# A new opening for an encoder step: the first weight block in half-size pieces scaled on ScalarE, the gain vectors on ScalarE's queue, and the remaining loads ordered behind the query weights

## The chip, the cores and the metric

The kernel runs on one core of one Trainium2 chip. The metric is the device time of one execution in microseconds (us); lower is better. Engine names are those of the profile: PE is TensorE, PEld its weight loads, DVE is VectorE, ACT is ScalarE, POOL is GpSimd, SP is SyncE, which issues most DMAs.

## The reference, cut to what matters

One step of a two-layer streaming encoder over 1024 prompt tokens and 8 x 16 sample tokens, width 1024, all in float32. The opening of a layer is a norm, a projection, and a norm of each head:

```python
def rmsnorm(x, g):
    y = xf * lax.rsqrt(jnp.mean(xf * xf, axis=-1, keepdims=True) + EPS)
    return (y * g.astype(jnp.float32)).astype(x.dtype)

def project_a(x, g_norm, w_qkv, g_q, g_k):
    qkv = rmsnorm(x, g_norm) @ w_qkv
    q, k, v = jnp.split(qkv, [N_HEADS * HEAD_DIM, (N_HEADS + N_KV_HEADS) * HEAD_DIM], axis=-1)
    q = rmsnorm(q.reshape(b, t, N_HEADS, HEAD_DIM), g_q)
    k = rmsnorm(k.reshape(b, t, N_KV_HEADS, HEAD_DIM), g_k)
```

Layer A then does a sliding-window attention with learned sinks, an output projection and a squared-ReLU MLP; layer B does the same with a shared K/V projection (`w_kv`, norm gain `g_kv`), a query projection (`w_q_b`) and an attention over more tokens.

## The kernel before, in words

The tokens lie in nine tiles of 128: tiles 0 to 7 are the prompt and tile ST (number 8) is the sample. A float32 product is made of three float32r matmuls: each operand is split into a high part (a rounded copy) and a low part (the rest), and high x high, high x low and low x high are added in PSUM (lines 182 to 184, three matmuls for each of eight 128-row blocks of the contraction, called k0 to k7 here).

The norm is folded in. Its gain is multiplied into the weights: `load_block` loads a 1024 x 512 weight block in four raw tiles of 512 KB, each with two of the eight k, and `split_g` makes of each k the high part, scaled by the gain column `gcol` (POOL, line 152, since `"g"` is in the layer's `eng` string), and the low part (DVE, line 155). The token's own scale is applied after the product. `prep_gains` loads five gain vectors as rows, transposes them on PE (line 1139) and copies them to `gcol` (DVE, line 1140). It has a PSUM pool of its own and runs ahead of everything else.

The names of the steps of a layer's attention (`attention`): `X(t)` loads tile t (line 1313). `N(t)` transposes it on PE (eight 128 x 128 transposes, line 175), splits the result into `hh` and `hl` (ACT line 109, DVE line 115) and makes the statistics (ACT line 166, DVE lines 167 and 1144, POOL line 1148). `K1(t)` is the key and value projection with the first weight block, `wkv`; its end (`kv_stage1`, lines 233 to 262) empties the PSUM tile with ACT (lines 241, 248, 249) and DVE (line 242). `K2(t)` transposes the keys (`ps_q<-ks`) and splits them into `KT`, of which two DMAs (lines 278, 279) make a swapped copy. `Q1(t, nb)` is the query projection with the second weight block (`wq[0]`); its end (`q_stage1`) makes `qn` and `qr` on ACT (lines 191, 192), and a power on POOL and a product on DVE (lines 203, 204) finish `qr`. In layer A there is one buffer of `qr`, in layer B two. `Q2(t, nb)` transposes `qr` into `qT`. `spill(t)` stores `hh` and `hl` to DRAM as `hTd` (line 1343), and `R(t)` reads them back much later. `sinks` loads the constant table `cst` and the sinks and makes five small DVE tiles of them (lines 1238 to 1256). `unit` works on the sample's caches (`kc`, `vc`). Layer A starts with tiles 0, 1 and ST, whose `K1` are woven k by k into three PSUM tiles; that of tile 0 is the only buffer of its kind ("m") and is used again by `Q1(0)`.

Nothing of the order is fixed by hand here: the tile framework's scheduler lists the instructions of each engine by a simulated timeline, starting from the order and the priorities in which they are written, so a change of the written order moves instructions elsewhere too. Each engine then runs its list strictly in order. DMAs of SP and of ACT share eight completion counters in turn; in the built program a DMA waits, on the engine that issues it, until the DMA that had the same counter before has landed, so about eight are in flight. `behind(a, b)` tells the scheduler to list b behind a; it adds no wait on the chip.

Of the kernel before, what the change touches and what calls it, by code (L numbers as in the profile page):

```python
# [75 lines left out]
class Build:  # L76
# [70 lines left out]
    def split_g(self, hi, lo, raw, g, k0):  # L147
        nc = self.nc
        for k in range(raw.shape[1]):
            s = self.gcol[:, g * KC + k0 + k : g * KC + k0 + k + 1]  # L150
            if "g" in self.engs:
                nc.gpsimd.tensor_scalar(hi[:, k], raw[:, k], s, 1.0, ALU.mult, ALU.mult)
# [2 lines left out]
            nc.vector.scalar_tensor_tensor(  # L155
                lo[:, k], raw[:, k], s, hi[:, k].bitcast(F32), ALU.mult, ALU.subtract
            )
# [20 lines left out]
    def proj(self, ps, ah, al, w, ks=range(KC)):  # L178
        nc = self.nc
        for k in ks:  # L180
            a, b = ah[k // 4][:, k % 4, :], al[k // 4][:, k % 4, :]
            nc.tensor.matmul(ps, a, w[:, 0, k, :], start=(k == 0), stop=False)  # L182
            nc.tensor.matmul(ps, a, w[:, 1, k, :], start=False, stop=False)  # L183
            nc.tensor.matmul(ps, b, w[:, 0, k, :], start=False, stop=(k == KC - 1))  # L184
# [943 lines left out]
    def prep_gains(self):  # L1128
        nc, I = self.nc, self.ins
        with ExitStack() as st:  # L1130
            self.psum_pools(st, "pg", dict(m=(1, 1)), dict(m="m"))
            tmp = self.pool(st, "tmpg")
            g = tmp.tile([5 * KC, P], F32, tag="g", name="g")
            for i, v in enumerate(
                (I["g_attn"][0], I["g_attn"][1], I["g_mlp"][0], I["g_mlp"][1], I["g_kv"])
            ):
                nc.sync.dma_start(g[i * KC : (i + 1) * KC, :], v.rearrange("(k p) -> k p", p=P))
            ps = self.psum("m", [P, 5 * KC], "ps_g")
            nc.tensor.transpose(ps, g, self.ident[0 : 5 * KC, 0 : 5 * KC])
            nc.vector.tensor_copy(self.gcol, ps)  # L1140
# [94 lines left out]
    def sinks(self, ring):  # L1235
        nc, I = self.nc, self.ins
        self.cst = ring.tile([P, C_W], F32, tag="cst", name="cst")
        nc.sync.dma_start(self.cst, I["consts"])
# [7 lines left out]
        for i in range(G):  # L1246
            nc.sync.dma_start(
                self.ssink[i * 32 : i * 32 + 32, :],
                sk[i : i + 13 : 4].partition_broadcast(32),
            )  # L1250
# [5 lines left out]
        nc.vector.tensor_tensor(self.susink, self.ssink, rsl, ALU.mult)  # L1256

    def attention(self, layer):
# [17 lines left out]
        with ExitStack() as st:  # L1276
# [27 lines left out]
            def X(t):  # L1304
                if A:
# [7 lines left out]
                nc.sync.dma_start(xr[t], x_src(t))  # L1313
# [475 lines left out]
```

## Time and profile before

| | |
|---|---|
| runs, median of 3 | 2394.24 us (2392.23 to 2396.98) |
| the profiled execution, its own time | 2396.21 us |
| its span in the trace, mean granted clock | 2394.4 us, 0.993 |
| busy shares | PE 97%, PEld 81%, DVE 68%, ACT 51%, POOL 23% |
| DMA | 385.88 MB, mean 161 GB/s |

The span runs from the first to the last instruction in the trace. PE is busy nearly all the time, so the places that matter are those in which PE waits or runs at a reduced clock. In a row of the timeline stand the start, the duration, the engine, the line, the operation with its output and inputs, the count of instructions merged, and in brackets the idle time just before with what ended it.

### The profile page before, as it was taken

Reading aid. Unit: us, or ns where it says so; the run is one execution under the profiler, and the core shown is the slowest. Engines: PE = TensorE matmul, PEld = TensorE weight load, DVE = VectorE, ACT = ScalarE, POOL = GpSimd, SP = SyncE. Lnnn points to the kernel's source line nnn. Section 1 sums busy time; section 2 is a strip of 40 time slices with the busy share of each in tenths; the row PEclk is TensorE's granted clock in tenths of the full one; section 3 lists DMA queues with packets and bytes.
Section 4 is the critical chain, followed back from the end, with each engine's and each line's share of the span. In section 5 each row is a group of like instructions: output and inputs, shape, how many; then the busy total and the mean of one; then the engine's idle time right before and its main releaser. Section 6 shows DMA issues by size and latency. Waiting matters only on the chain.

```text
span 2394.4 us, 33443 instructions
## 1 busy us (share of the span) xinstructions
PE 2315.4 (97%) x11621; PEld 1932.2 (81%) x11621; DVE 1629.9 (68%) x3002; ACT 1212.0 (51%) x2415; POOL 542.5 (23%) x836
## 2 busy tenths in 40 slices
PE   7999999899999999999999999998999999999999
PEld 6777877788888878888777788876888888888887
DVE  6787786755655767776577876877655555777674
ACT  3776675555555432332277666665555555323321
POOL 4343332312212100000243444444111211000000
PEclk9998999999999999999999999999999999999999
DMA  7345545344433874342754655555433445734332
GB/s 253 119 132 166 171 155 193 103 150 157 145 129 141 324 245 141 112 141 100 246 155 114 197 163 169 166 167 171 141 133 137 154 141 202 275 138 158 114 115 115
DMA packets 218393, 385.88 MB, mean 161 GB/s; under 512 B 50344, under 2 KB 125040, under 8 KB 211056
## 3 DMA queue, kind: packets, MB, share of 16 engines
q1 hardware_dynamic: 195152, 307.18, 39.0%
q0 software_dynamic: 21776, 71.84, 7.8%
q10 hardware_dynamic: 1296, 4.72, 0.5%
q8 instruction: 92, 1.51, 0.3%
q14 instruction: 77, 0.63, 0.1%
HBM read 246.47 MB, written 136.14 MB: 160 GB/s over the span
## 4 chain that ended last, share of the span: by engine, by line
PE 81%; DVE 7%; DMA 6%; ACT 3%; issue 2%; POOL 1%; SPq 0%; POOLq 0%; ACTq 0%; DVEq 0%
PE ps_x L711 9%; PE ps_x L713 9%; PE ps_x L712 9%; PE ps_y L713 7%; PE ps_y L712 7%; PE ps_y L711 7%; PE ps_mm L182 3%; PE ps_mm L184 3%; PE ps_mm L183 3%; PE ps_tr L289 2%; PE ps_mm L143 2%; PE ps_mm L145 2%; PE ps_mm L144 2%; PE ps_s L713 1%; PE ps_s L712 1%
## 5 line engine op out<-in xcount | busy, mean ns | idle before, releaser
L109 ACT CAST w<-r 128x2048 fp32r<-128x2048 f32 x56 | 107.1, 1913 | 321.6 <-PE ps_y L713 210.6
L711 PE MATMUL ps_x<-w,s 128*128 128x512 f32 x512 | 199.5, 390 | 4.3 <-DVE x L1017 2.2
L713 PE MATMUL ps_x<-w,s 128*128 128x512 f32 x512 | 199.4, 389 | 0.0
L712 PE MATMUL ps_x<-w,s 128*128 128x512 f32 x512 | 199.2, 389 | 0.0
L182 PE MATMUL ps_mm<-w,hh 128*128 128x512 f32 x432 | 174.2, 405 | 9.7 <-DMA hh<-hTd 3.3
L184 PE MATMUL ps_mm<-w,hl 128*128 128x512 f32 x432 | 174.1, 404 | 1.7 <-DMA hl<-hTd 1.6
L183 PE MATMUL ps_mm<-w,hh 128*128 128x512 f32 x432 | 172.5, 400 | 1.6 <-DVE w L155 1.6
L109 ACT CAST s<-s 128x2048 fp32r<-128x2048 f32 x56 | 107.2, 1914 | 121.3 <-DMA s<-hd 112.2
L115 DVE TENSOR_TENSOR w<-r,w 128x2048 fp32r<-128x2048 f32 x56 | 128.2, 2289 | 51.0 <-ACT w L109 51.0
L711 PE MATMUL ps_x<-sx,w 128*128 128x512 f32 (+1 forms) x408 | 157.9, 387 | 3.8 <-ACT hc L830 2.9
L1017 DVE TENSOR_TENSOR x<-ps_y,x 128x512 f32<-128x512 f32 x136 | 92.3, 687 | 99.8 <-PE ps_y L713 99.8
L713 PE MATMUL ps_x<-sx,w 128*128 128x512 f32 (+1 forms) x408 | 154.1, 378 | 0.0
L712 PE MATMUL ps_x<-sx,w 128*128 128x512 f32 (+1 forms) x408 | 154.1, 378 | 0.0
L109 ACT CAST w<-ru 128x512 fp32r<-128x512 f32 (+1 forms) x160 | 110.0, 708 | 85.4 <-PE ps_y L712 32.0
L713 PE MATMUL ps_y<-w,s 128*128 128x512 f32 x384 | 149.5, 389 | 0.0
L711 PE MATMUL ps_y<-w,s 128*128 128x512 f32 x384 | 149.4, 389 | 0.0
L712 PE MATMUL ps_y<-w,s 128*128 128x512 f32 x384 | 149.4, 389 | 0.0
L115 DVE TENSOR_TENSOR s<-s 128x2048 fp32r<-128x2048 f32 x56 | 128.0, 2286 | 30.4 <-ACT s L109 30.3
L115 DVE TENSOR_TENSOR ptl<-ps_tr,pth 128x512 fp32r<-128x512 f32 x180 | 122.6, 685 | 24.2 <-ACT pth L109 18.6
L115 DVE TENSOR_TENSOR w<-ru,w 128x512 fp32r<-128x512 f32 (+1 forms) x160 | 126.4, 792 | 11.2 <-ACT w L109 11.2
L115 DVE TENSOR_TENSOR wq<-ru,wq 128x1024 fp32r<-128x1024 f32 x32 | 39.7, 1240 | 132.2 <-ACT wq L109 132.2
L109 ACT CAST pth<-ps_tr 128x512 fp32r<-128x512 f32 x180 | 104.8, 595 | 45.6 <-PE ps_tr L289 33.2
(279 smaller groups left out, 6570.6 us busy)
## 6 DMA issues: line engine op xcount, KB each, us to landing
s<-hd SPq DMA_DIRECT2D x56, 1024.0 KB, 4.7
ru<-in_w_up SPq DMA_DIRECT2D x64, 512.0 KB, 3.8
r<-in_w_down SPq DMA_DIRECT2D x32, 1024.0 KB, 5.8
hd<-hc POOLq DMA_DIRECT2D x128, 256.0 KB, 2.7
hd<-hs POOLq DMA_DIRECT2D x96, 256.0 KB, 2.5
x<-xd SPq DMA_DIRECT2D x41, 512.0 KB, 4.5
o<-oTd SPq DMA_DIRECT2D x52, 256.0 KB, 3.9
hTd<-hh SPq DMA_DIRECT2D x36, 256.0 KB, 3.9
```

The source lines that it names most:

```text
L109: a = nc.scalar.copy(hi, src)
L115: return a, e.tensor_tensor(lo, src, hi.bitcast(F32), ALU.subtract)
L143: nc.tensor.matmul(ps, oh[:, k, :], w[:, 0, k, nn], start=(k == 0), stop=False)
L144: nc.tensor.matmul(ps, oh[:, k, :], w[:, 1, k, nn], start=False, stop=False)
L145: nc.tensor.matmul(ps, ol[:, k, :], w[:, 0, k, nn], start=False, stop=(k == 3))
L182: nc.tensor.matmul(ps, a, w[:, 0, k, :], start=(k == 0), stop=False)
L183: nc.tensor.matmul(ps, a, w[:, 1, k, :], start=False, stop=False)
L184: nc.tensor.matmul(ps, b, w[:, 0, k, :], start=False, stop=(k == KC - 1))
L711: a = mm(ps, ah, bh, start=first, stop=False, skip_group_check=True)
L712: mm(ps, ah, bl, start=False, stop=False, skip_group_check=True)
L713: return a, mm(ps, al, bh, start=False, stop=last, skip_group_check=True)
L1017: tt(xs[t][:, N[n]], ps, xs[t][:, N[n]], ALU.add)
```

## The change

In words:

- `prep_gains` is split up. `load_gains` issues three DMAs (two gain matrices at once, and `g_kv`) on ACT's queue; `turn_gains`, the transpose and the copy to `gcol`, is written behind `N(0)`.
- In layer A's first weight block each raw tile is loaded by two DMAs of 256 KB, one for each k, and its high part is made on ACT (`first=True`) and no longer on POOL.
- `X(0)` and `N(0)` are written ahead of the first weight load. The raw tile of ST's tokens lies in another pool (`qT`).
- `self.gate` names the last weight load (later the loads of tiles 2 and 3). The spills of tiles 0, 1 and ST, the loads of `cst`, the sinks, `kc`, `vc` and `gb` are listed behind it. `sinks` is written behind the `K1` steps, and its DVE operations are listed behind the last matmul of `proj`.
- `Q2(0, 0)` is written ahead of `K2(1)`, and in layer A `X(2)` and `X(3)` ahead of `spill(0)`. The move of `Q2(0, 0)`, and the gate on spills, caches and `gb`, hold for layer B as well.

```diff
-    def load_block(self, dst, w, n0, g, ks=range(0, KC, 2)):
+    def load_block(self, dst, w, n0, g, ks=range(0, KC, 2), first=False):
...
-            nc.sync.dma_start(raw, wr[:, k0 : k0 + 2, n0 : n0 + 512])
-            self.split_g(dst[:, 0, k0 : k0 + 2, :], dst[:, 1, k0 : k0 + 2, :], raw, g, k0)
+            step = 1 if first else 2
+            for k in range(0, 2, step):
+                self.gate = nc.sync.dma_start(
+                    raw[:, k : k + step], wr[:, k0 + k : k0 + k + step, n0 : n0 + 512]
+                )
+            self.split_g(dst[:, 0, k0 : k0 + 2, :], dst[:, 1, k0 : k0 + 2, :], raw, g, k0, first)
...
-            if "g" in self.engs:
+            if "g" in self.engs and not first:
                 nc.gpsimd.tensor_scalar(hi[:, k], raw[:, k], s, 1.0, ALU.mult, ALU.mult)
             else:
                 nc.scalar.activation(hi[:, k], raw[:, k], AF.Copy, scale=s)
...
-            nc.tensor.matmul(ps, b, w[:, 0, k, :], start=False, stop=(k == KC - 1))
+            self.lp = nc.tensor.matmul(ps, b, w[:, 0, k, :], start=False, stop=(k == KC - 1))
...
+        d = nc.sync.dma_start(kc, cache_k[2 * bp : 2 * bp + 2, :, j, :].rearrange("b k d -> k b d"))
+        self.behind(self.gate, d)
...
+        d = nc.sync.dma_start(vc, cache_v[2 * bp : 2 * bp + 2, :, j, :].rearrange("b k d -> k b d"))
+        self.behind(self.gate, d)
...
+    def load_gains(self, pool):
         nc, I = self.nc, self.ins
+        g = pool.tile([5 * KC, P], F32, tag="pvt", name="g", bufs=1)
+        n = 2 * KC
+        for i, v in enumerate((I["g_attn"], I["g_mlp"])):
+            nc.scalar.dma_start(g[i * n : (i + 1) * n, :], v.rearrange("l (k p) -> (l k) p", p=P))
+        nc.scalar.dma_start(g[2 * n :, :], I["g_kv"].rearrange("(k p) -> k p", p=P))
+        return g
+
+    def turn_gains(self, g):
+        nc = self.nc
+        ps = self.psum("m", [P, 5 * KC], "ps_g")
+        nc.tensor.transpose(ps, g, self.ident[0 : 5 * KC, 0 : 5 * KC])
+        nc.vector.tensor_copy(self.gcol, ps)
...
-        nc.sync.dma_start(self.cst, I["consts"])
+        self.behind(self.gate, nc.sync.dma_start(self.cst, I["consts"]))
...
-        nc.vector.tensor_tensor(self.susink, self.ssink, rsl, ALU.mult)
+        z = nc.vector.tensor_tensor(self.susink, self.ssink, rsl, ALU.mult)
+        self.behind(self.lp, z)
...
+                if A and t == ST:
+                    xr[t] = apool.tile([P, D], F32, tag="qT", name="x", bufs=2)
...
+                d = nc.sync.dma_start(xr[t], x_src(t))
+                if A and t in (2, 3):
+                    self.behind(self.gate, d)
+                    self.gate = d
...
+                        d = nc.sync.dma_start(self.hTd[t][:, v, c], hts[t][v][z].bitcast(F32))
+                        if t in (0, 1, ST):
+                            self.behind(self.gate, d)
...
             if A:
+                g = self.load_gains(apool)
                 X(0)
-                self.load_block(wkv, wkv_src, kv0, gkv, [0])
+                N(0)
+                self.turn_gains(g)
+                self.load_block(wkv, wkv_src, kv0, gkv, [0], True)
                 X(1)
-                N(0)
-                self.load_block(wkv, wkv_src, kv0, gkv, [2])
+                self.load_block(wkv, wkv_src, kv0, gkv, [2], True)
                 X(ST)
                 N(1, "pt")
-                self.load_block(wkv, wkv_src, kv0, gkv, [4, 6])
+                self.load_block(wkv, wkv_src, kv0, gkv, [4, 6], True)
                 N(ST, "p")
...
                 weave(K1(0), K1(1, "s"), K1(ST, "s"))
+                self.sinks(ring)
...
+            if A:
+                X(2)
+                X(3)
             spill(0)
             run(Q1(0, 0))
             K2(0)
             spill(1)
             run(Q1(1, 0, "s"))
+            Q2(0, 0)
             K2(1)
             spill(ST)
             run(Q1(ST, 0, "s"))
             K2(ST)
-            X(2)
-            Q2(0, 0)
+            if not A:
+                X(2)
             N(2)
-            X(3)
+            if not A:
+                X(3)
             Q2(1, 0)
```

What the scheduler makes of it, at three places. A row gives the line, the operation, the output and inputs and the size; a count at its end stands for equal neighbours.

The first place is the opening. SP's queue before, from the first token tile on; `raw` are the weight tiles (four of `wkv`), `cst` and the sinks stand ahead of the sample's tokens:

```order
L1313 DMA x<-in_x_prompt 128x1024 x2
L127 DMA raw_267<-in_w_qkv_a 128x2x512
L127 DMA raw<-in_w_qkv_a 128x2x512 x2
L127 DMA raw_305<-in_w_qkv_a 128x2x512
L590 DMA gk<-in_g_k_a 128x64
L590 DMA gq<-in_g_q_a 128x64
L1238 DMA cst<-in_consts 128x596
L1240 DMA sink<-in_sink_a 128x16
L1313 DMA x<-in_x_sample 128x1024
L1247 DMA ssink<-in_sink_a 32x4x1 x4
```

And SP's queue now, from the same tile on; `raw` of 128x512 are pieces of `wkv`, those of 128x2x512 are tiles of `wq[0]`:

```order
L1325 DMA x<-in_x_prompt 128x1024
L129 DMA raw<-in_w_qkv_a 128x512 x2
L1325 DMA x<-in_x_prompt 128x1024
L129 DMA raw_258<-in_w_qkv_a 128x512 x2
L1325 DMA x<-in_x_sample 128x1024
L129 DMA raw<-in_w_qkv_a 128x512 x2
L129 DMA raw_298<-in_w_qkv_a 128x512 x2
L596 DMA gk<-in_g_k_a 128x64
L596 DMA gq<-in_g_q_a 128x64
L129 DMA raw<-in_w_qkv_a 128x2x512
```

Tile ST moved ahead of half of `wkv`, and `wq[0]` follows at once, where `cst`, the sinks and the first spills stood (they now follow `wq[0]`, with tiles 2 and 3 between the sinks and the spills). At the same place ACT's list before, which makes only statistics (`junk`) and high parts of tokens (`hh`) until the values of `K1` (`VS`):

```order
L166 ACTIVATE junk,xssq<-x 128x1024
L109 CAST hh<-ps_n 128x512
L166 ACTIVATE junk,xssq<-x 128x1024
L109 CAST hh<-ps_n 128x512 x3
L166 ACTIVATE junk,xssq<-x 128x1024
L109 CAST hh<-ps_n 128x512 x2
L241 ACTIVATE VS<-ps_mm,rx 128x4x64 x2
```

And now, where the pieces of `wkv` are scaled between them (`w<-raw,gcol`):

```order
L170 ACTIVATE junk,xssq<-x 128x1024
L109 CAST hh<-ps_n 128x512 x2
L158 ACTIVATE w<-raw,gcol 128x512 x2
L170 ACTIVATE junk,xssq<-x 128x1024
L158 ACTIVATE w<-raw_258,gcol 128x512
L109 CAST hh<-ps_n 128x512
L158 ACTIVATE w<-raw_258,gcol 128x512
L109 CAST hh<-ps_n 128x512
L170 ACTIVATE junk,xssq<-x 128x1024
L158 ACTIVATE w<-raw,gcol 128x512 x2
L109 CAST hh<-ps_n 128x512
L158 ACTIVATE w<-raw_298,gcol 128x512
```

Eight scalings came to ACT, the last two behind the sample's high parts. On PE the three `K1` before ended one after the other, 22 matmuls of tile ST behind the other two; now the last nine matmuls are three of each tile, and 6 matmuls stand between the end of `K1(0)` and `Q1(0)`.

The second place is ACT around the first `Q2` of layer A; before, the copy `qr` of tile 1 stands behind the statistics of tile 2 and a part of `kt`:

```order
L191 ACTIVATE qn<-ps_mm 128x512
L166 ACTIVATE junk,xssq<-x 128x1024
L109 CAST kt_640<-ps_q 64x2x128
L192 COPY qr<-ps_mm 128x512
L109 CAST qT<-ps_q 64x4x128
```

Now the `qr` of tile 1 is copied ahead of the first `qT`:

```order
L195 ACTIVATE qn<-ps_mm 128x512
L196 COPY qr<-ps_mm 128x512
L109 CAST qT<-ps_q 64x4x128
L109 CAST KT<-ps_q 64x2x128
L109 CAST qT<-ps_q 64x4x128
L195 ACTIVATE qn<-ps_mm 128x512
```

The copy of tile 1's `qr` now stands ahead of the casts of `Q2(0, 0)`, and on PE the four transposes of `Q2(0, 0)`, which read the one buffer of `qr`, stand behind 15 of the 24 matmuls of `Q1(ST)`, where before they stood behind all 24.

The third place is SP in layer B's opening, from the output of the sample's values to the load of tile 2 (`xd_113`); before:

```order
L261 DMA out<-v_11064 128x256
L278 DMA KT<-KT 64x4x128
L279 DMA KT<-KT 64x4x128
L259 DMA out<-kw 128x256
L278 DMA KT<-KT 64x4x128
L279 DMA KT<-KT 64x4x128
L1313 DMA x<-xd_113 128x1024
```

And now:

```order
L265 DMA out<-v_11058 128x256
L509 DMA kc<-in_cache_k_b 128x2x64
L512 DMA vc<-in_cache_v_b 128x2x64
L282 DMA KT<-KT 64x4x128
L283 DMA KT<-KT 64x4x128
L509 DMA kc<-in_cache_k_b 128x2x64
L263 DMA out<-kw 128x256
L282 DMA KT<-KT 64x4x128
L1325 DMA x<-xd_113 128x1024
L283 DMA KT<-KT 64x4x128
```

The load of tile 2 moved ahead of the last `KT` copy. On PE in layer B, before, the query projections of tiles 0, 1 and ST took turns (12, 12 and 6 matmuls, and then the rest of each), with 4 transposes of `qr` right ahead of tile 2's; now the 24 matmuls of `Q1(0)` stand in one piece, and 12 score matmuls stand ahead of tile 2's transposes.

More of the change, by code (lines that the diff above doesn't have):

```diff
@@ L145, in wo_proj, with split_g @@
             nc.tensor.matmul(ps, ol[:, k, :], w[:, 0, k, nn], start=False, stop=(k == 3))
-    def split_g(self, hi, lo, raw, g, k0):
+    def split_g(self, hi, lo, raw, g, k0, first=False):
         nc = self.nc
@@ L1126, in prep_bias @@
             nc.sync.dma_start(self.biasSd[0:KV].rearrange("j p c -> p j c"), big)
-    def prep_gains(self):
+    def load_gains(self, pool):
         nc, I = self.nc, self.ins
[L1130 to L1140, printed above, removed]
+        g = pool.tile([5 * KC, P], F32, tag="pvt", name="g", bufs=1)
[9 more added lines that the diff above has]
+        nc.vector.tensor_copy(self.gcol, ps)
     def token_scales(self, t, need_r):
@@ L1201, in run @@
             self.kT8d = [dram([P, KV, P], f"kT8d{l}") for l in range(2)]
-            self.prep_gains()
             flat = lambda a: a.rearrange("b s h d -> (b s) (h d)")
@@ L1237, in sinks @@
         self.cst = ring.tile([P, C_W], F32, tag="cst", name="cst")
-        nc.sync.dma_start(self.cst, I["consts"])
+        self.behind(self.gate, nc.sync.dma_start(self.cst, I["consts"]))
         self.sink = ring.tile([P, H], F32, tag="sink", name="sink")
-        nc.sync.dma_start(self.sink, I["sink_a"][0].partition_broadcast(P))
+        self.behind(self.gate, nc.sync.dma_start(self.sink, I["sink_a"][0].partition_broadcast(P)))
         self.usink = ring.tile([P, H], F32, tag="usink", name="usink")
-        nc.vector.tensor_tensor(self.usink, self.sink, self.cst[:, C_ISL : C_ISL + H], ALU.mult)
+        z = nc.vector.tensor_tensor(self.usink, self.sink, self.cst[:, C_ISL : C_ISL + H], ALU.mult)
+        self.behind(self.lp, z)
         nc.vector.tensor_scalar(self.usink, self.usink, -1.0, None, ALU.mult)
@@ L1246, in sinks @@
         for i in range(G):
-            nc.sync.dma_start(
+            d = nc.sync.dma_start(
                 self.ssink[i * 32 : i * 32 + 32, :],
@@ L1250, in sinks @@
             )
+            self.behind(self.gate, d)
         self.nslope = ring.tile([P, KV], F32, tag="nslope", name="nslope")
-        nc.vector.tensor_scalar(self.nslope, self.cst[:, C_SLS : C_SLS + KV], -1.0, None, ALU.mult)
+        z = nc.vector.tensor_scalar(self.nslope, self.cst[:, C_SLS : C_SLS + KV], -1.0, None, ALU.mult)
+        self.behind(self.lp, z)
         self.susink = ring.tile([P, KV], F32, tag="susink", name="susink")
@@ L1255, in sinks @@
         nc.vector.reciprocal(rsl, self.nslope)
-        nc.vector.tensor_tensor(self.susink, self.ssink, rsl, ALU.mult)
+        z = nc.vector.tensor_tensor(self.susink, self.ssink, rsl, ALU.mult)
+        self.behind(self.lp, z)
     def attention(self, layer):
@@ L1342, in spill @@
                     for v in range(2):
-                        nc.sync.dma_start(self.hTd[t][:, v, c], hts[t][v][z].bitcast(F32))
+                        d = nc.sync.dma_start(self.hTd[t][:, v, c], hts[t][v][z].bitcast(F32))
+                        if t in (0, 1, ST):
+                            self.behind(self.gate, d)
             def R(t):
@@ L1548, in attention @@
             nc.vector.tensor_tensor(gkq8, gk, gq8, ALU.mult)
-            if A:
-                self.sinks(ring)
-            else:
+            if not A:
                 self.biasB = {}
@@ L1589, in attention @@
             K2(ST)
-            X(2)
-            Q2(0, 0)
-            N(2)
-            X(3)
+            if not A:
+                X(2)
+            N(2)
+            if not A:
+                X(3)
             Q2(1, 0)
@@ L1653, in attention @@
                 if s == 10:
-                    nc.sync.dma_start(self.gb, I["g_mlp"][layer].partition_broadcast(P))
+                    d = nc.sync.dma_start(self.gb, I["g_mlp"][layer].partition_broadcast(P))
+                    self.behind(self.gate, d)
                 q, n = s + 2, s + 3
```

5 lines of the change are left out of this document (1 added, 4 removed).

## The prediction, made before the changed kernel was run

> **What bounds the kernel.** I read the page first, for the shares and the chain that ended last.
>
> ```profile
> span 2394.4 us, 33443 instructions
> PE 2315.4 (97%) x11621; PEld 1932.2 (81%) x11621; DVE 1629.9 (68%) x3002; ACT 1212.0 (51%) x2415; POOL 542.5 (23%) x836
> PE 81%; DVE 7%; DMA 6%; ACT 3%; issue 2%; POOL 1%; SPq 0%; POOLq 0%; ACTq 0%; DVEq 0%
> ```
>
> PE is the bound: time is won only where it waits or is slow, and what is won early is kept, since all later waits hang on work and not on a clock. So I asked second for PE's waits in the first 120 us (total, times, longest), and third for its busy time and granted clock (PEclk) around the first projection.
>
> ```profile
> PE ps_g L1139 <- DMA g<-in_g_kv: 4.1, 1, 4.1
> PE ps_mm L182 <- POOL w L152: 3.0, 1, 3.0
> PE ps_n L175 <- DMA x<-in_x_prompt: 2.2, 1, 2.2
> PE ps_q L225 <- DVE qr L204: 1.8, 1, 1.8
> PE ps_mm L183 <- DVE w L155: 1.6, 1, 1.6
> ...
> 13.20:15.50 2.30, 0.73 (x2) 0.30 (x2) 2.30 (x4) 0.00 (x0) 2.30 (x3) 0.71 0.42 148
> 15.50:21.10 5.60, 5.59 (x13) 4.42 (x14) 5.13 (x12) 1.15 (x2) 2.71 (x3) 0.51 0.53 187
> 21.10:40.40 19.30, 19.30 (x90) 15.98 (x89) 12.10 (x22) 3.82 (x9) 9.77 (x14) 1.00 1.04 393
> ```
>
> PE waits for tokens, then for the scaled weights (POOL, then DVE). It is full from 15.5 us, but at a clock of 0.51 until 21.1: 13 matmuls in 5.6 us, 0.43 us each. Only from there to 40.4 is it full at clock 1.00. Fourth, the timeline gives the stations.
>
> ```profile
> 0.74 0.38 SPq L1172 DMA_DIRECT2D eye<-in_eye  x1
> 2.93 0.83 SPq L1313 DMA_DIRECT2D x<-in_x_prompt  x2
> 6.46 1.06 ACT L166 ACTIVATE junk<-x 128x1024 bf16<-128x1024 f32 x1 [4.44 <-DMA x<-in_x_prompt]
> 6.57 3.65 PE L175 MATMUL ps_n<-identr,x 128*128 128x128 f32 x16 [2.21 <-DMA x<-in_x_prompt]
> 7.69 0.59 ACT L109 CAST hh<-ps_n 128x512 fp32r<-128x512 f32 x1
> 8.18 1.06 ACT L166 ACTIVATE junk<-x 128x1024 bf16<-128x1024 f32 x1
> 10.16 1.36 POOL L152 TENSOR_SCALAR w<-raw,gcol 128x512 fp32r<-128x512 f32 x2 [1.72 <-DMA raw<-in_w_qkv_a]
> ...
> 22.50 0.39 PE L182 MATMUL ps_mm<-w,hh 128*128 128x512 f32 x1
> 23.18 0.39 PE L182 MATMUL ps_mm<-w,hh 128*128 128x512 f32 x1
> 29.13 0.47 ACT L241 ACTIVATE VS<-ps_mm,rx 128x256 fp32r<-128x256 f32 x1 [3.77 <-PE ps_mm L184]
> ...
> 40.44 0.38 PE L225 MATMUL ps_q<-identr,ks 128*128 128x128 f32 x2
> ```
>
> Three full-clock matmuls take 0.68 us (22.50 to 23.18), 0.227 each. The 24 of `Q1(0)` end at 40.44, so the 72 of the three `K1` end at 40.44 - 24 x 0.227 = 35.0 us.
>
> **The opening, step by step.** SP issues tile 0 right behind `eye`, at 0.74 + 0.38, about 1.15, and no longer at 2.93; it landed 3.53 us after its issue (6.46), so now at 4.7. Sixteen cold transposes took 3.65, so eight take 1.8: PE is done with tile 0 at 6.5. The gain loads are three issues on ACT of about 0.35 (as on SP) ahead of a table load that ran from 0.73 to 2.01 and would end at 3.1; that lies before 4.7 and costs nothing; were the tokens there by 3, it would cost at most 1.1. Tile 1 was at work at 8.18, at most 4.8 after its issue; now it is issued at about 2.4 with two 256 KB pieces ahead of it, and the DMAs move 0.37 MB per us in the stretch below, 1.4 us for both. I take 8.0, between 7.2 and 8.6.
>
> ```profile
> 5.00:6.00 1.00, 0.00 (x0) 0.00 (x0) 0.00 (x0) 0.00 (x0) 0.00 (x0) 1.00 0.98 373
> ...
> L785 ACT ACTIVATE hc<-hc 128x512 f32<-128x512 f32 x120 | 75.6, 632 | 3.6
> L152 POOL TENSOR_SCALAR w<-raw,gcol x16: 684/692/1120, 10.2 to 33.7; 128x512 fp32r<-128x512 f32 x16
> L155 DVE SCALAR_TENSOR_TENSOR w<-raw,gcol,w x16: 737/1171/1178, 10.9 to 34.9; 128x512 fp32r<-128x512 f32 x16
> ```
>
> The nearest row for a piece scaled on ACT is the activation of the same size from SBUF, 0.63 us (POOL 0.69). ACT's list to the last piece: three statistics of 1.25 (1.06 and its read-out), six `hh` of 0.59, eight pieces of 0.63 = 12.3 us, from 4.7 to 17.0. DVE's low parts fall from 1.17 to 0.74 while POOL is idle: eight of 0.74 and six `hl` of 0.69 are 10.1, so DVE follows ACT; with two parts of `wq[0]` listed between, it has the last one at about 20.
>
> PE then: transposes of tile 1 from 8.0 to 9.8, seven matmuls of `K1` (the first two k of tile 0 by 9.7 on DVE) of 0.43 to 12.8, tile ST's transposes to about 14.2. The full clock came 5.6 us after PE went into its unbroken stretch at 15.5; from 8.0 that gives 13.6. Left are 65 matmuls of 0.227, 14.8 us, for which k4 to k7 are there in time (17 to 20): `K1` ends at 29.0, not 35.0. Gain 6.0. Bounds: if the stretch counts only from the end of ST's transposes, the full clock comes at about 19.8, 6 us at half speed cost 3: gain 3.0. A clock 2 us earlier adds 1.0: gain 7.0.
>
> By the Trainium skill, "TensorE: Matmul & The Clock Gate", Part 1, the array is gated to half clock by default and released after one busy window of about 3.4 us: an estimate from it would put the full clock at 11.4 and the gain at 7.0. The row's 5.6 us are more than the page's window, so I keep 6.0.
>
> `Q1(0)` needs the one PSUM tile of `K1(0)`. Before, 27 matmuls lay between (`K1(0)` ended at 29.1, as `VS` at 29.13 shows); now 6, that is 1.4 us, and emptying takes 0.47 on ACT, 0.47 on DVE and two copies of about 0.38 on ACT, with tile 1's 0.47 between: 2.2 us. A new wait of 0.8, cost 0.7. `wq[0]` comes in its cover: its last tile waits for the slot freed at 20, lands some 4 us later and is split by 27.
>
> **Moved at no cost.** The spills (12 DMAs), `cst`, the sinks, `kc`, `vc` and `gb` go behind `wq[0]`. `spill(0)` must land before tile 2's `hh` is written, which was at 54 us; it has some 20 us. The cover of `cst` and the sinks is thin; see the first rival. Tiles 2 and 3 are issued at about the same time as before, so a full queue is all they meet.
>
> **`Q2(0, 0)`.** PE waited 1.8 us for tile 1's `qr`:
>
> ```profile
> 52.06 0.60 PE L225 MATMUL ps_q<-identr,qr 128*128 128x128 f32 x4
> 53.89 0.58 ACT L192 COPY qr<-ps_mm 128x512 f32<-128x512 f32 x1
> 54.59 0.69 DVE L204 TENSOR_TENSOR qr<-qr,qrs 128x512 f32<-128x512 f32 x1
> ```
>
> The copy at 53.89 could not be made until the transposes of 52.06 had read the one buffer. They now stand nine matmuls earlier, so this wait should go. Of its 1.8 us I count half, 0.9 (0 to 1.8): `ps_s`, which needs `qT` and the copied keys, is late next.
>
> **Layer B.** The load of tile 2 is stuck in SP's queue behind the key copies:
>
> ```profile
> 1196.17 0.38 PE L225 MATMUL ps_q<-identr,ks 128*128 128x128 f32 x2
> 1198.79 0.59 SPq L278 DMA_DIRECT2D KT<-KT  x1
> 1200.16 0.55 SPq L1313 DMA_DIRECT2D x<-xd  x1
> 1203.71 1.07 PE L175 MATMUL ps_n<-identr,x 128*128 128x128 f32 x8 [2.82 <-DMA x<-xd]
> ...
> 1205.00:1210.00 5.00, 5.00 (x25) 4.30 (x25) 4.50 (x14) 2.61 (x5) 0.55 (x1) 0.66 0.89 301
> ```
>
> Now it passes one key copy (saves 0.6), but tile 1's key transposes stand four transposes and seven matmuls later on PE (about 2.1), and ACT puts two `qT` casts between the `KT` casts. The issue comes at about 1201.0 and the tile at 1204.5, 0.8 later. In the wait PE now does 12 score matmuls, about 1.4 us of work. Net gain 0.6; between a loss of 2 (the scores wait as well) and a gain of 4.5 (the 2.82, and 5 us at 0.66, if the wait goes).
>
> Sum: 6.0 - 0.7 + 0.9 + 0.6 = 6.8. The profiled execution took 2396.21 us, 1.8 around its span, and stands 1.97 above the median 2394.24; less 6.8 it would take 2389.4, and the median 2387.4. About 0.2% (4.8 us) is what a measurement tells from no change, so the forecast lies a little beyond it.
>
> **Rivals.** First, a new wait for the sinks. They now follow `wq[0]`, and on DVE the five sink operations stand ahead of the `VS` that frees `Q1(0)`'s PSUM.
>
> ```profile
> 11.41 4.43 SPq L1247 DMA_DIRECT2D ssink<-in_sink_a  x4
> 21.08 0.16 DVE L1256 TENSOR_TENSOR susink<-ssink,rsl 128x4 f32<-128x4 f32 x1 [0.47 <-DMA ssink<-in_sink_a]
> ...
> cst<-in_consts SPq DMA_DIRECT2D x1, 298.0 KB, 9.9
> ```
>
> Issued until 15.84 they landed at 21.08, 5.2 later. Issued until 23 they land at 28.2, just when DVE gets there. At the 9.9 us that `cst` took it is 33: 4.7 us of wait, and half clock after it, which cost 1.7 in layer B (5 us at 0.66). Gain 6.8 - 6.4 = 0.4: 2393.8. It decides once the sinks land after 29.
>
> Second, ACT or the clock holds the opening: full clock at 19.8, gain 6.8 - 3.0 = 3.8, or less if ACT's pieces take as long as POOL's worst, 1.12 (eight times 0.49 more, 3.9, of which PE's work ahead hides most). 2390.4 to 2392.
>
> Third, slower: in layer B `Q1(0)` now stands in one piece, at about 1182.9. Before, the last two weight tiles came late and PE filled in with other tiles.
>
> ```profile
> 1187.94 3.39 POOL L152 TENSOR_SCALAR w<-raw,gcol 128x512 fp32r<-128x512 f32 x4 [1.78 <-DMA raw<-in_w_q_b]
> 1193.34 0.75 DVE L155 SCALAR_TENSOR_TENSOR w<-raw,gcol,w 128x512 fp32r<-128x512 f32 x1
> ```
>
> If they come no earlier, PE reaches k7 at 1187.7 and waits until 1194.1: 6.4 and 1.7 at half clock, 8.1 against the 6.2 of layer A: 2396.1. Against it: 3 MB of spills no longer stand ahead of them. It decides if they are issued later than about 1179 (they were at 1181.2).
>
> **Chances.** The forecast with its own range, 2383 to 2389.4: 0.60. The second rival 0.19, the first 0.12, the third 0.09, of which about half passes 2399. So faster by over 0.2% 0.60, the same 0.35, slower 0.05. The range takes the best ends of layers A and B in part (gain 11.2, 2383) and reaches to the first rival's end less its rarest part (2393.5).
>
> **What the profile will show.** Right: PE's first key transposes (`ps_q<-ks`) at about 35 us in place of 40.44; first `K1` matmul before 10; clock 1.00 from about 14; no wait for `qr` L204 of 1.8; in layer B a wait for `x<-xd` of 2 to 3 us as before, and none for `w` in `Q1(0)`. Wrong: a wait of PE or DVE on `ssink` or `cst` near 28; PE waiting for ACT's pieces between 14 and 20; a clock near 0.5 until 18 or later; PE waiting for DVE `w` near 1186. The whole sum is wrong if the time gained at 35 us is not there at 350, when the re-sorted rows of layer A's attention are done.

## The result: 0.6% slower, and the profile after

| | before | after |
|---|---|---|
| median | 2394.05 us (2391.69 to 2396.98, 6 runs) | 2410.81 us (2400.61 to 2412.56, 6 runs) |
| ratio, 95% interval | | 1.0058 [1.0038, 1.0077] |
| span of the profiled execution | 2394.4 us | 2408.9 us |
| windows of half clock in it (below) | 9 | 17 |

The forecast was 2387.4 us, 0.2% faster; the kernel is 0.6% slower. A window is one step, of 3.41 us, of the grid on which PE's clock changes; the grid is worked out below. The page of after, busy times and the chain that ended last:

```profile
PE 2325.7 (97%) x11621; PEld 1941.2 (81%) x11621; DVE 1627.4 (68%) x3002; ACT 1217.1 (51%) x2423; POOL 541.6 (22%) x828
PE 84%; DMA 7%; DVE 5%; ACT 3%; issue 1%; POOL 1%; SPq 0%; ACTq 0%; DVEq 0%; POOLq 0%
```

PE is still the bound, and it is busy 10.3 us longer (2325.7 against 2315.4) with the same 11621 matmuls, so most of the loss is not waiting: matmuls ran slower. The timeline of after in the opening shows the gain and its end:

```profile
5.80 1.06 ACT L170 ACTIVATE junk<-x 128x1024 bf16<-128x1024 f32 x1 [2.27 <-DMA x<-in_x_prompt]
8.49 1.34 ACT L158 ACTIVATE w<-raw,gcol 128x512 fp32r<-128x512 f32 x2
9.97 0.48 PE L186 MATMUL ps_mm<-w,hh 128*128 128x512 f32 x1
...
21.01 1.85 SPq L1254 DMA_DIRECT2D ssink<-in_sink_a  x4
27.30 0.39 PE L188 MATMUL ps_mm<-w,hl 128*128 128x512 f32 x1
30.33 0.16 DVE L1265 TENSOR_TENSOR susink<-ssink,rsl 128x4 f32<-128x4 f32 x1 [3.18 <-DMA ssink<-in_sink_a]
30.92 0.37 ACT L252 COPY kw<-ps_mm 128x256 f32<-128x256 f32 x1 [3.34 <-DVE VS L246]
31.68 0.76 PE L186 MATMUL ps_mm<-w,hh 128*128 128x512 f32 x1 [3.99 <-ACT kw L253]
39.81 0.38 PE L229 MATMUL ps_q<-identr,ks 128*128 128x128 f32 x2
```

`K1` begins at 9.97 and ends at 27.7, 7.3 us sooner than the 35.0 before. Then DVE waits 3.18 us for the last sink load (issued until 22.86, landed at 30.33), `VS` and `kw` of tile 0 stand behind it, and PE waits 3.99 us for the PSUM tile. The same stretch by windows (busy time and count of each engine, then granted clock, DMA share, GB/s):

```profile
26.93:30.35 3.42, 0.76 (x4) 0.30 (x2) 0.24 (x4) 0.47 (x1) 0.00 (x0) 1.00 0.39 146
30.35:33.76 3.41, 2.08 (x5) 1.72 (x6) 1.90 (x6) 1.02 (x3) 1.02 (x1) 0.50 1.03 407
33.76:37.17 3.41, 3.41 (x9) 2.64 (x9) 1.43 (x5) 0.66 (x2) 1.01 (x1) 0.50 1.05 402
```

After a stretch with 0.76 us of work the clock is 0.50 until 37.17. `Q1(0)`, running from 31.68, loses 2.7 us by that. Of the 7.3 us, 0.6 are left: the first key transposes stand at 39.81 in place of 40.44.

Layer B's opening, PE's waits from 1150 to 1240 us, then rows of the timeline:

```profile
PE ps_n L179 <- DMA x<-xd: 6.4, 2, 4.4
PE ps_mm L187 <- DVE w L159: 1.4, 2, 0.7
PE ps_sn L400 <- DVE qT L115: 0.7, 1, 0.7
PE ps_mm L186 <- POOL w L156: 0.5, 1, 0.5
...
1187.87 1.82 SPq L129 DMA_DIRECT2D raw<-in_w_q_b  x2
1209.32 0.38 PE L229 MATMUL ps_q<-identr,ks 128*128 128x128 f32 x2
1212.77 0.60 SPq L282 DMA_DIRECT2D KT<-KT  x1
1213.42 0.60 SPq L1325 DMA_DIRECT2D x<-xd  x1
1218.95 1.97 PE L179 MATMUL ps_n<-identr,x 128*128 128x128 f32 x8 [4.40 <-DMA x<-xd]
```

Counted from the last matmul of layer A's MLP (1140.1 before, 1146.2 now), tile 2's load is issued after 67.2 us and not after 60.1. PE waits 4.40 us for it (2.82 before) and 1.9 us in all for weights, which it did not before. What the load stands behind begins with `kc`, the sample's cached keys (the first row is of before, the others of after):

```profile
1174.26 0.38 SPq L505 DMA_DIRECT2D kc<-in_cache_k_b  x1
...
1199.55 0.73 SPq L509 DMA_DIRECT2D kc<-in_cache_k_b  x1
1203.53 0.29 DVE L529 TENSOR_TENSOR kc<-kc,gq 128x128 f32<-128x128 f32 x1 [2.54 <-DMA kc<-in_cache_k_b]
1208.44 1.64 POOL L207 TENSOR_TENSOR qrs<-qms,mhalf 128x8 f32<-128x8 f32 x1 [1.68 <-DVE qms L205]
1212.38 0.37 ACT L109 CAST KT<-ps_q 64x256 fp32r<-64x256 f32 x1
```

`kc` was issued 34.2 us behind the MLP and is now issued 53.3 us behind it, after the twelve spills. DVE waits 2.54 us for its landing, where before it did not wait for it. From that operation to the key copy at 1212.77 the rows follow each other with no gap over 0.1 us: the keys' power (`krs`) on POOL, the keys and the sums of `qn` on DVE, the power for `qr` on POOL, `qr` and the low part of `qT` on DVE, then the second `qT` cast and the second `KT` cast on ACT. Then the clock:

```profile
1211.36:1214.77 3.41, 2.51 (x16) 1.84 (x14) 3.03 (x9) 2.18 (x5) 0.00 (x0) 1.00 0.17 40
1214.77:1218.18 3.41, 0.00 (x0) 0.00 (x0) 3.14 (x16) 2.23 (x11) 2.45 (x2) 0.50 0.66 223
1218.18:1221.59 3.41, 2.64 (x13) 2.64 (x14) 0.00 (x0) 2.55 (x6) 1.16 (x4) 0.50 0.37 100
1221.59:1225.00 3.41, 3.41 (x13) 2.65 (x13) 2.37 (x10) 2.09 (x7) 1.27 (x3) 0.50 1.00 288
```

The rest of the loss lies in neither opening. At 338 us, where layer A's attention ends, PE waits exactly as long before and after, and pays another price. The waits of before, after, and a third kernel (run e6 below, whose layer A is that of after); then the windows, in the same order:

```profile
339.33 0.49 PE L296 MATMUL ps_pv<-pth,VS 128*128 128x512 f32 x1 [2.31 <-ACT pth L109]
...
339.52 0.49 PE L300 MATMUL ps_pv<-pth,VS 128*128 128x512 f32 x1 [2.31 <-ACT pth L109]
...
345.20 0.50 PE L300 MATMUL ps_pv<-pth,VS 128*128 128x512 f32 x1 [2.31 <-ACT pth L109]
```

```profile
335.01:338.42 3.41, 2.01 (x16) 1.69 (x14) 2.51 (x6) 3.41 (x5) 1.82 (x2) 1.00 0.55 160
338.42:341.83 3.41, 2.50 (x16) 1.95 (x17) 3.41 (x10) 2.17 (x6) 0.30 (x1) 1.00 0.53 168
...
337.54:340.96 3.42, 1.44 (x9) 1.03 (x10) 3.42 (x8) 2.83 (x5) 0.85 (x1) 1.00 0.57 175
340.96:344.37 3.41, 2.85 (x13) 2.12 (x11) 3.41 (x9) 2.21 (x6) 1.18 (x2) 0.50 0.20 64
344.37:347.78 3.41, 3.41 (x14) 3.03 (x13) 3.13 (x8) 3.36 (x12) 0.46 (x1) 0.50 0.69 199
...
341.39:344.80 3.41, 1.50 (x12) 1.18 (x9) 3.01 (x8) 3.41 (x5) 1.82 (x2) 1.00 0.40 131
344.80:348.21 3.41, 2.59 (x15) 1.73 (x15) 3.41 (x7) 1.54 (x4) 0.81 (x1) 1.00 0.60 172
```

The clock changes only on a grid: within one execution of these traces every half-clock stretch begins and ends at the same offset modulo 3.4133 us (0.51 in the trace of before, 3.04 in that of after). The stretches are 3.41, 6.83 or 10.24 us long. Before, the wait of 2.31 us lay across two windows, which kept 2.01 and 2.50 us of work, and nothing happened. After, 1.98 us of it fell into one window, 1.44 us of work were left there, and the next two windows ran at half clock. In e6 1.50 us were left, and it stayed full.

### The profile page after: what moved, and what is told of

Its sections match the earlier page's. It is cut to its first block, busy times and chain, and to the rows that moved or that the text cites. A ratio compares the mean times of both kernels' runs of the same rounds, so it can differ in the third digit from the quotient of the medians.

```text
span 2408.9 us, 33417 instructions
## 1 busy us (share of the span) xinstructions
PE 2325.7 (97%) x11621; PEld 1941.2 (81%) x11621; DVE 1627.4 (68%) x3002; ACT 1217.1 (51%) x2423; POOL 541.6 (22%) x828
## 4 chain that ended last, share of the span: by engine, by line
PE 84%; DMA 7%; DVE 5%; ACT 3%; issue 1%; POOL 1%; SPq 0%; ACTq 0%; DVEq 0%; POOLq 0%
PE ps_x L717 9%; PE ps_x L719 9%; PE ps_x L718 9%; PE ps_y L719 7%; PE ps_y L717 7%; PE ps_y L718 7%; PE ps_mm L186 3%; PE ps_mm L188 3%; PE ps_mm L187 3%; PE ps_tr L293 3%; PE ps_mm L147 2%; PE ps_mm L149 2%; PE ps_mm L148 2%; PE ps_pv L301 1%; PE ps_pv L300 1%
## 5 line engine op out<-in xcount | busy, mean ns | idle before, releaser
L115 DVE TENSOR_TENSOR wq<-ru,wq 128x1024 fp32r<-128x1024 f32 x32 | 39.7, 1240 | 132.3 <-ACT wq L109 132.3
```

Source lines behind the costliest of these rows:

```text
L115: return a, e.tensor_tensor(lo, src, hi.bitcast(F32), ALU.subtract)
```

## The experiments

Each is compared with the kernel before on the same chip. The runs lie on four chips (e1 to e4, e5 to e8, e9 and e10, e11 and e12), so rows are compared by their ratios. The last column counts the windows of half clock in the one profiled execution (the last microseconds, when the kernel drains, left out), with its span.

| run | kernel | median us (runs) | before | ratio, 95% interval | windows, span |
|---|---|---|---|---|---|
| e1 | the change again | 2413.51 (6) | 2396.03 | 1.0063 [1.0046, 1.0080] | 15, 2404.6 |
| e2 | layer B as before | 2401.40 (12) | 2396.03 | 1.0023 [1.0009, 1.0036] | 10, 2404.6 |
| e3 | before + layer B's part | 2404.56 (12) | 2396.03 | 1.0033 [1.0021, 1.0045] | 12, 2403.3 |
| e4 | sinks late | 2407.34 (7) | 2396.03 | 1.0046 [1.0027, 1.0065] | 11, 2398.0 |
| e5 | layer B without `Q2` moved | 2408.69 (9) | 2398.59 | 1.0042 [1.0026, 1.0058] | 18, 2409.1 |
| e6 | layer B without the gates | 2406.49 (11) | 2398.59 | 1.0038 [1.0026, 1.0050] | 12, 2405.7 |
| e7 | e2 and e4 together | 2397.43 (12) | 2398.59 | 1.0003 [0.9991, 1.0015] | 9, 2392.2 |
| e8 | e7, and `kc`, `vc` early | 2395.28 (12) | 2398.59 | 0.9994 [0.9983, 1.0005] | 10, 2394.3 |
| e9 | e8, and `Q2` unmoved in A | 2392.40 (11) | 2395.81 | 0.9980 [0.9969, 0.9991] | 9, 2388.4 |
| e10 | before + `Q2` moved in A | 2400.80 (11) | 2395.81 | 1.0016 [1.0004, 1.0028] | 10, 2402.3 |
| e11 | e9, `kc`'s work behind the weights' | 2388.02 (5) | 2397.07 | 0.9970 [0.9958, 0.9981] | 9, 2389.1 |
| e12 | e9, but `kc`, `vc` late | 2394.19 (12) | 2397.07 | 0.9988 [0.9977, 1.0000] | 12, 2391.0 |

**e1: the change again.** No edit.

> The changed kernel once more, for the spread of its times and for a second trace. In the first trace the half clock begins and ends only at multiples of 3.41 us (17 such windows of half clock, against 9 before), and 6 of the 8 windows more stand at seams that the change does not touch (338, 379, 897, 1358, 1676 and 1686 us). Theory 'grid' (whether a stall of 2 to 3 us falls inside one window or across two decides): if the grid's offset is drawn anew in each execution, this trace shows another offset than 3.04 us, other seams at half clock, and times spread between about 2400 and 2412. Theory 'places' (the loss is in the edited places alone): the times lie within 2 us of 2410.8 and the same 17 windows are there.

The offset was 2.30, not 3.04, and the set of windows another one: 2 at 340 us as in after, none at 382 or 901, but 1 at 1159 and 2 at 1354. The times spread over 2406 to 2416, where 2400 to 2412 was expected. So the offset is drawn anew, as the theory "grid" has it; over all 14 traces it lies between 0.02 and 3.29. But all 12 runs of the change lie 6 to 20 us over the median of before, so luck is not all: most of the loss belongs to the kernel.

**e2, e3: layer B undone, and layer B alone.**

```diff
 e2, on after
             run(Q1(1, 0, "s"))
-            Q2(0, 0)
+            if A:
+                Q2(0, 0)
...
             if not A:
                 X(2)
+                Q2(0, 0)
...
-                        if t in (0, 1, ST):
+                        if A and t in (0, 1, ST):
                             self.behind(self.gate, d)
```

The gates on `kc`, `vc` and `gb` are tied to layer A in the same way; e3 adds to before what e2 takes from after.

> Layer B's opening as it was before (Q2(0,0) after X(2), no order for the spills, cache loads and gb behind the weights), layer A's opening as changed. Theory 'places': layer B's opening lost 8.3 us between 1157 and 1300, so 2410.8 - 8.3 = 2402.5. Theory 'grid' with a free offset: the same 8 us from here, but 3 to 10 us more or less from the untouched seams: 2394 to 2406. Rival that layer B's order costs nothing: 2410 again.

> The kernel before, with layer B's part of the change alone (Q2(0,0) moved, spills, cache loads and gb ordered behind the weights), layer A untouched. Theory 'places': 2394 + 8.3 = 2402.4, with the wait for tile 2's row (x<-xd) at 4.4 us or so instead of 2.8, about 2 us of waits for weights in Q1(0), and 3 more half-clock windows between 1190 and 1225. Rival that the loss needs layer A's shift: within 2 us of 2394.

Undone, layer B gives back 0.0040, 9.6 us (of 2400); alone it costs 0.0033, 7.9 us. Both agree with the 8.3 us expected. The trace of e3 has the same waits with layer A untouched, so the loss does not come from running 6 us ahead:

```profile
1207.24 0.59 SPq L1317 DMA_DIRECT2D x<-xd  x1
...
1212.46 1.97 PE L175 MATMUL ps_n<-identr,x 128*128 128x128 f32 x8 [4.08 <-DMA x<-xd]
```

That issue stands 67.2 us behind the end of layer A's MLP, as in after. And by e2 layer A's part alone is slower than before, by 0.0023, where the prediction had it faster.

**e4: the sinks' DVE operations behind `Q1(1)`.**

```diff
-                self.sinks(ring)          # loads and five DVE operations
+                self.sinks(ring)          # the loads alone
...
             run(Q1(1, 0, "s"))
+            if A:
+                self.sinks2(ring)         # the five DVE operations
```

> The changed kernel with the five small VectorE operations on the sinks moved behind Q1(1) in VectorE's order, so that VS and kw of tile 0 no longer stand behind the wait for ssink (3.2 us). Theory 'sinks held it': Q1(0) begins when K1 ends, at about 28 instead of 31.7, the two half-clock windows at 30.3 to 37.2 go, and the first transpose of ks stands at 34 to 35 instead of 39.8: 5 to 7 us less, 2404 to 2406. Rival 'given back': tile 2's rows and the weights are late next (the waits at 54 to 58 us grow by as much), so that the attention of layer A ends at 326 us as before, and the time stays within 2 us of 2410.8.

```profile
34.93 0.38 PE L229 MATMUL ps_q<-identr,ks 128*128 128x128 f32 x2
...
42.85 0.47 POOL L529 TENSOR_TENSOR kc<-kc,gq 128x128 f32<-128x128 f32 x1 [3.82 <-DMA kc<-in_cache_k_a]
44.31 0.49 DVE L260 TENSOR_TENSOR kw<-kw,krs 128x256 f32<-128x256 f32 x1 [4.56 <-POOL krs L259]
...
46.73:53.18 6.45, 2.88 (x19) 2.56 (x19) 4.79 (x11) 5.14 (x11) 3.98 (x4) 0.77 0.94 278
```

The wait is gone, the keys stand at 34.93, where I had forecast 35. Part is given back: `kc`, now behind the spills, lands late; POOL waits for it ahead of `krs`, DVE for `krs`, and from 46.73 to 53.18 PE works 2.88 of 6.45 us. Both theories were half right: by the ratios the gain is 0.0017, 4 us, where 5 to 7 were expected.

**e5, e6: the two halves of layer B's part.** e5 undoes only the move of `Q2(0,0)` in layer B (the first two hunks of e2), e6 only the order behind `self.gate`, the gates:

```diff
 e6, on after
-                        if t in (0, 1, ST):
+                        if A and t in (0, 1, ST):
                             self.behind(self.gate, d)
...
-        self.behind(self.gate, d)
+        if not layer:
+            self.behind(self.gate, d)
```

> The changed kernel with Q2(0,0) of layer B back at its old place, behind X(2); the order of layer B's spills, cache loads and gb behind the weights stays. Two causes of layer B's 8 to 10 us are told apart. Theory 'Q2': without its transposes between tile 2's load and tile 2's transposes nothing covers the load, so its place is the cause: 2411.8 (median of the changed kernel's 12 runs so far) falls to 2402 to 2404, and the half clock at 1211 to 1225 goes. Theory 'order of loads': Q1(0) in one piece meets late weights and the KT writes keep the row of tile 2 back on SP, whatever Q2 does: 2409 or more, with tile 2's load still issued 7 us later, counted from the first row transposes of the layer.

> The counterpart: layer B's spills, cache loads and gb without the order behind the weights, Q2(0,0) at its new place. Theory 'Q2': 2409 or more. Theory 'order of loads': 2402 to 2404. If each costs about half, both kernels lie at 2406 to 2407.

Over e2 (1.0023), where neither is there, the gates alone (e5) cost 0.0019, the move alone (e6) 0.0015, both 0.0040: about half each, the third case of the expectation for e6. The intervals are about 0.0012 to 0.0016 either way, so which is larger is not settled. The rows of e5 (first two) and e6 show two different waits:

```profile
1212.42 0.60 SPq L1325 DMA_DIRECT2D x<-xd  x1
1216.04 1.04 PE L400 MATMUL ps_sn<-KT,qT 128*128 128x128 f32 x6 [2.24 <-DVE qT L115]
...
1204.25 0.37 SPq L1327 DMA_DIRECT2D x<-xd  x1
1209.72 0.44 PE L229 MATMUL ps_q<-identr,ks 128*128 128x128 f32 x2 [1.69 <-DVE ks L271]
```

With the gates, tile 2's load comes 65.1 us behind the MLP; without them, 57.1, earlier than before's 60.1. Then the keys are late instead.

**e7, e8: layer B as before with the sinks late; then `kc` and `vc` early too.** e7 joins the edits of e2 and e4, e8 adds, for `kc` and `vc`:

```diff
-        self.behind(self.gate, d)
```

> Layer B's opening as before and the sinks' VectorE operations behind Q1(1). If the two parts add: 2411.8 - 10.4 (layer B as before: 2401.4) - 4.5 (sinks late: 2407.3) = 2397, level with the kernel before at 2396, since in layer A a new gap of 6.7 us at 46.5 to 53.2 has given back half of what the sinks gave.

> As the run with layer B as before and the sinks late, and the loads of the cached keys and values (kc, vc) no longer behind weights and spills. In the sinks' run kc was issued at 38.9 instead of 25.7 us, POOL's operation on it waited 3.8 us for the landing, krs of the third tile stood behind it, and VectorE waited 4.6 us for krs. Theory 'kc holds the Q chain': the gap at 46.5 falls from 6.7 to 2 to 3 us and its two half-clock windows go, 4 to 7 us less than with kc late: 2390 to 2393, which beats the kernel before (2396). Rival 'the rows of tile 2 are next': the gap stays over 5 us, and the time at 2396 to 2397.

e7 came out level with before, as added up. e8 gained 0.0009, about 2 us and not the 4 to 7 expected: the gap at 46 us shrank (1.8 us idle from 45 to 60), but PE still had 3.3 us of waits at 80 to 110 us, where the view of before lists none, and `kc`'s operations now stood between POOL's scalings (e11).

**e9, e10: `Q2(0,0)` of layer A.** e9 is e8 with it back behind `K2(ST)`; e10 is before with only this moved.

```diff
 e10, on before
             run(Q1(1, 0, "s"))
+            if A:
+                Q2(0, 0)
...
             X(2)
-            Q2(0, 0)
+            if not A:
+                Q2(0, 0)
```

> As the run with kc early, and Q2(0,0) of layer A at its old place too, so that of the whole change only the opening is left (first tile and weights in pieces, norm vectors on the other queue, spills, sinks' loads and gb behind the query weights), with the sinks' operations late and kc early. Every kernel with Q2(0,0) early in layer A had TensorE's later rows in another order and 3.4 us of small waits at 85 to 115 us, where the kernel before has 0.2. Theory 'Q2 reorders layer A': these waits go, the wait of 1.8 us for qr comes back in part, and the time is 2 to 3 us under the run with kc early: a ratio of 0.998 to 0.9985 to the kernel before (2391 to 2393 where that is 2396), so faster than before. Rival 'the waits are the price of running 6 us ahead': they stay at 85 to 115, and the ratio stays at 0.9994.

> The kernel before with one thing changed: Q2(0,0) of layer A at its new place, ahead of K2(1). Theory 'Q2 reorders layer A': waits of about 3.4 us appear at 85 to 115 us and the 1.8 us wait for qr goes: 1 to 3 us slower, a ratio of 1.0005 to 1.0012. Rival 'the waits come from running ahead': none there, and the time is 0 to 1.8 us less.

PE's waits from 80 to 125 us in e10; in e9 and in before the view lists none:

```profile
PE ps_pv L296 <- ACT pth L109: 1.6, 1, 1.6
PE ps_s L345 <- DVE qT L115: 0.6, 1, 0.6
PE ps_n L175 <- DVE oT L324: 0.6, 2, 0.3
PE ps_utp L570 <- ACT sp L566: 0.4, 1, 0.4
PE ps_s L345 <- DMA KT<-KT: 0.2, 1, 0.2
```

The move alone brings them, 3.4 us, without the changed opening. The theory holds, and the price, 0.0016, is a little over the expected range. e9 is faster than before.

**e11, e12: `kc`'s work on POOL.** e11 is e9 with POOL's first `kc` operation listed behind the last scaling of `wq[0]` (`hi0`); e12 is e9 without the edit that e8 added.

```diff
 e11, on e9
-        self.eng("c").tensor_tensor(kp, kc, gq8.unsqueeze(1).to_broadcast([P, 2, HD]), ALU.mult)
+        z = self.eng("c").tensor_tensor(kp, kc, gq8.unsqueeze(1).to_broadcast([P, 2, HD]), ALU.mult)
+        if self.hi0 is not None and not layer:
+            self.behind(self.hi0, z)
```

> As the run with Q2(0,0) at its old places, and POOL's operations on the early kc put behind POOL's eight scalings of the query weights. There kc's operations (0.8, 0.3 and 0.9 us, and 0.9 for the next unit) stood between the scalings, the last scaling ended at 28.8, VectorE took VS of tile 0 only at 29.9, and TensorE waited 2.0 us at 29 to 31 for kw. Theory 'POOL': that wait falls to under 1 us and the time by 1 to 2 us, a ratio of 0.9973 to 0.998. Rival: the wait moves on to qr, and the ratio stays at 0.998.

> As the run with Q2(0,0) at its old places, but kc and vc behind the weights and spills again, as the change has them. Theory 'kc holds krs': POOL's operation on kc waits for the landing at about 42 us ahead of krs of the third tile, VectorE stands 4 us behind it, TensorE gets a gap of 3 to 6 us between 40 and 55, and the time is 2 to 5 us longer: a ratio of 0.9988 to 1.000. Rival, that kc late costs nothing where Q2 stands at its old place: 0.998 or, with POOL's scalings free of kc, 0.9975.

e9's wait, then the same group in e11 (total, times, longest):

```profile
31.15 0.47 PE L186 MATMUL ps_mm<-w,hh 128*128 128x512 f32 x1 [1.99 <-ACT kw L253]
...
PE ps_mm L186 <- ACT kw L253: 1.8, 2, 0.9
```

e11 came out a little better than expected. e12's time is the expected one, its gap is not: DVE waits 4.7 us for `krs` behind `kc`, but PE only 2.3 us, for `qr` at 51 us, where 3 to 6 were expected. With 0.9970 e11 is the fastest of all: the opening gains 7.2 us, with `sinks`' operations, `kc`, `vc`, `Q2(0, 0)` and layer B taken out of the change, and the spills, `cst`, the sinks' loads and `gb` of layer A still behind the weights.

## Why the prediction was wrong, point by point

The opening gained what I had forecast. What failed is "Moved at no cost": the sinks and `kc` landed late, ahead of engines that take their work in order, and what that and the moves of `Q2(0, 0)` brought was in the sum at 0 or as a small gain. The steps in one chain, each the difference of two neighbouring kernels, in us of 2400. Each has an uncertainty of 3 to 5 us, so the small ones rest on the waits shown and not on the times alone.

| step | kernels | forecast | measured |
|---|---|---|---|
| the opening itself | e11 against before | 5.3 faster (6.0, less 0.7 for the PSUM tile) | 7.2 faster |
| sinks ahead of `VS` | e2 - e7 | 0 | 4.8 slower |
| `kc`, `vc` behind the weights | e7 - e8; e12 - e11 | 0 | 2.2; 4.3 slower |
| `Q2(0,0)` early in layer A | e8 - e9; e10 | 0.9 faster | 3.4; 3.8 slower |
| layer B's part | e1 - e2; e3 | 0.6 faster | 9.6; 7.9 slower |

The 2.2 are less than the 4.3 because the early `kc` at first stood between POOL's scalings; from e9 to e11, where it no longer does, 2.4 are won.

- **The opening was right in its size.** The tokens landed at 5.80 (forecast 4.7) and a scaling on ACT took 0.71 to 0.73 (0.63), but `K1` still began at about 10 and ended at 27.7 in after, 28.7 in e1 and 29.2 in e2 (29.0). The full clock did not come 5.6 us into an unbroken stretch, as I had read the row, but on the grid: in e1, e2 and e4 at 12.5 to 13.5, with six or seven matmuls at half speed (forecast seven, until 13.6), in after at 9.87, ahead of the first. That after's `K1` ended at 27.7 is in part such luck.
- **The failed step there is the landing of the sinks.** I took the 5.2 us of the trace of before and had them land at 28.2, "just when DVE gets there". They took 7.5. The first rival named the place, the mechanism, the price (4.7 of wait, 4.0 measured; 1.7 of half clock, 2.7 measured) and the point where it decides (29; it was 30.33), and had 0.12. A cover that ends "just when" should have had even odds.
- **"Moved at no cost" was wrong for `kc`.** I asked what memory the moved loads must free and by when, and not which engine takes the load next: in layer A POOL, in order, ahead of `krs`; in layer B DVE, ahead of everything that the key copies need.
- **`Q2(0,0)`:** the 1.8 us wait for `qr` did go. I counted only it, and named `ps_s` as late next. In e10 PE waits from 45 to 60 us for `hh` (1.3), `hl` (0.7) and `qT` (0.3) instead. And the move changed PE's order for hundreds of rows behind it (e10 and before still differ at 350 us); the 3.4 us of waits at 80 to 125 us were nowhere in the sum.
- **Layer B is the largest error.** The step "the issue comes at about 1201.0, 0.8 later" was 7.1 later, counted from the MLP's end. (Its own terms, 2.1 less 0.6, make 1.5 later and not 0.8.) I followed PE. I had the seven matmuls and four transposes right (2.1 us) and left out what else happens ahead of the key transposes: `Q1(0)` in one piece met the last two weight tiles, issued 41.6 us behind the MLP as before (41.2), and waited 1.9 us, and a half-clock window cost 1.7. That is the third rival's mechanism, at 3.6 in place of its 8.1. But it did not set the issue. In e3 no half-clock window falls ahead of the key transposes and they come sooner, 61.5 us behind the MLP where after has 63.1, and the issue stands at the same 67.2. In both, DVE's wait for `kc` ends 57.3 us behind the MLP, and the chain of rows shown with the result leads from there to the issue; its other input, `qn`, was there 1.1 us earlier in after and 2.7 us earlier in e3. So here too the failed step is "Moved at no cost", together with the two `qT` casts, which I had named between the `KT` casts and priced at nothing: the second `KT` cast begins 2.4 us behind the first, where before it was 1.0. No run moves `kc` alone in layer B, so this is read from the rows; e5 and e6 settle only that the gates and the move cost about half each.
- **The clock.** "What is won early is kept, since all later waits hang on work and not on a clock" was wrong. Later waits cost by where they fall on the grid. After has eight windows more at half clock; where PE works through one it loses 1.7 us, up to 13.7 in all, against 14.5 us between the two spans. Six more stand far from the edited places (338 to 385, 900, 1361 and 1680 us), three more in layer B's opening, one more in layer A's first 100 us, and two of before's, at 195 us, are not there. Which waits are hit is chance (e1 has 15 windows, in part elsewhere), and a change far ahead shifts them all. The granted clock, on record for each run, shows the average: 0.9925 over the 24 runs of before with e1, 0.9892 over the 12 of the change. A window is worth 0.0007 of it, so by estimate about 10 windows against 15, some 8 us of the loss. The medians above have that price in them.
- **The test that I named held.** I had said that the sum is wrong if the time gained at 35 us is not there at 350. In after 7.3 us were gained at the end of `K1`, 0.6 at the key transposes, and at the last `ps_pv` of layer A (387.35; 384.06 before) after is 3.3 us behind. In e4 the 5.5 us gained at the key transposes are 2.9 there.

## What to carry to other kernels

When loads or small operations are moved "out of the way", ask for each who takes it next and what stands behind that taker in its queue: here a few tiny operations on sinks and a cache in layer A cost about as much as the whole opening gained. A moved step that a scheduler re-sorts is not a local edit, so try it by itself and read the waits far behind it. With stalls of 2 to 3 us spread over a kernel, one profile is one draw: compare medians of many runs and use the trace for causes.

## What the runs showed of the hardware

In 14 traces, 9742 windows of 3.413 us laid on each trace's own offset: of the full-clock windows in which PE was busy under 1.5 us, 75 of 75 were followed by half clock; from 1.5 to 2.0 us, 31 of 110; from 2.0 to 2.5, 5 of 204; above, 1 of 9190. From half clock, all 94 windows that were busy for at least 3.25 us led back to full, and none of 28 under 2.5 us did. So a wait of 2.31 us was enough when 1.98 us of it fell into one window, and the same wait across two cost nothing.

The Trainium skill, "TensorE: Matmul & The Clock Gate", Part 1, gives a free-running window of 3413 ns; these traces agree. The same page of the Trainium skill, "Why this matters for your kernels", asks for no idle gap over about 3 us; here 2.31 us sufficed when most of it fell into one window, and the measurement decides.

The times spread as well: 24 runs of the kernel before on one chip lay between 2389.53 and 2403.62 us, more than the whole effect of most of these edits. The longer ones have the lower granted clock (correlation -0.72), so half clock is a part of the spread; that the offset alone makes it is not shown.

Four loads of 0.5 KB each needed 7.5 us from the last issue to the landing, where the 256 KB pieces of weights took a median of 5.8 us from issue to landing in the first 45 us of the same trace.
